# Operand sums of the seven-product gate in the feed-forward stage: traced between gate and up of the first tile pair, from high plus low parts

## The chip, the cores and the metric

The kernel runs on one core of one Trainium2 chip. The metric is the device time of one execution, in microseconds (us). The core has a matrix engine (PE, with its weight loads as PEld), a vector engine (DVE), an activation engine (ACT), a general engine (POOL) and a queue that issues transfers (SP). Matmuls write PSUM banks; everything else lives in SBUF.

## The reference, cut to what matters

Two layers; each has a mixer (three kinds of attention), then the feed-forward stage, then a small embedding stage. Sequence 512, model width 1024, feed-forward width 2816. The change lies in the feed-forward stage:

```python
hn = rms_norm(h, norm_ffn[i])
h = h + (jax.nn.silu(hn @ w_ffn_gate[i]) * (hn @ w_ffn_up[i])) @ w_ffn_down[i]
```

## The kernel before

**Number format.** Every f32 operand of a matmul is split into a high part (a copy to f32r, by ACT) and a low part (whole minus high, by DVE or POOL), and every product is three matmuls (`mm3`): high x high (L223), high x low (L224), low x high (L225).

**Norm.** `norm_T` takes four token tiles of 128 rows (tt 0 to 3), each in two halves of the width (kh 0 and 1). Row statistics run on ACT (squares, L313) and POOL (L322, L335, L336), DVE scales (L369, tile `xn`), PE transposes into a PSUM bank (L382, `xnT`; two such banks), ACT writes the high part (L387) and DVE the low part (L390) of `xT`. In the feed-forward stage ACT also copies the whole from the same bank into f32 tiles `xF` (L393, 8 copies a layer).

**Pairs.** `feed_forward` walks eleven pairs of 128 feed-forward columns (`fp`). Pair 0 computes gate and up directly: 96 matmuls of 256 columns each, first for tokens 0 to 255, then for 256 to 511. From pair 1 on the gate comes from `seven`: seven products of quadrants in place of eight (order 1, 7, 5, 2, 6, 4, 3; 12 matmuls each, 84 in all, tile `st`). Products 1, 2 and 4 read `xT` itself. Products 7, 5, 6 and 3 read sums of the four quadrants of the normed input, quadrant (t, kh) being token half t and width half kh:

X7 = (0,0) - (1,0), X5 = (1,0) + (1,1), X6 = X5 - (0,0), X3 = (0,1) - X6.

`operand_sums` makes them once a layer, each as a whole (DVE, L409, tile `Xw`), a high part (ACT, L411) and a low part (DVE, L412).

**Weights.** Weights land in `wraw` (four buffers). For the direct pairs each is split by `halves` into `whl` (five buffers): high by ACT (L199), low by POOL or DVE in turn (L202). In `seven` the right-hand sides are split at L445 (ACT) and L446 (POOL for products 1, 2, 3, DVE for the others), after differences on DVE (L431, tile `T`). After up, DVE multiplies gate and up (L1246), ACT and POOL split the result (L1247, L1248, tile `hid`).

**Order.** The order on each engine is fixed before the run. Among the instructions whose inputs and buffers are ready in the framework's modelled time, an engine takes the one traced earliest; `prio(n)` moves one n places forward. So later steps run early where an engine would be idle, and what is traced earlier goes first where two are ready. Tiles of `utile` share 15 buffers. In the run itself every engine keeps its order and waits.

Of the kernel before, what the change touches and what calls it, by code (L numbers as in the profile page):

```python
# [10 lines left out]
F32 = mybir.dt.float32  # L11
# [3 lines left out]
AF = mybir.ActivationFunctionType  # L15
ALU = mybir.AluOpType
# [3 lines left out]
P = 128  # L20
S = 512
# [21 lines left out]
def hybrid_trunk_kernel(  # L43
# [12 lines left out]
    te, ve, se, ge = nc.tensor, nc.vector, nc.scalar, nc.gpsimd  # L56
# [5 lines left out]
    def f(ap):  # L62
        return ap.bitcast(F32)
# [8 lines left out]
    def bank(tag, shape=(P, 512), dt=F32, name=None):  # L72
        bufs = {"d": 2, "s": 3, "t": 2, "o": 1}[tag]
        return ps.tile(list(shape), dt, name=name or f"ps_{tag}", tag=tag, bufs=bufs)

    def utile(shape, dt=F32R, name="u"):

        return upool.tile(list(shape), dt, name=name, tag="u", bufs=15)
# [12 lines left out]
    def etile(name="e"):  # L91
        return upool.tile([P, 512], F32, name=name, tag="e", bufs=4)
# [4 lines left out]
    def ptile(name="p"):  # L97
        return upool.tile([P, 512], F32, name=name, tag="p", bufs=6)
# [6 lines left out]


    OFE, OFN, OFP = 100, 50, 200
    KEEP = 150

    def weave(*streams):  # L110

# [8 lines left out]
    def run(*gens):  # L120
        for g in gens:
            for _ in g:
                pass
# [5 lines left out]
    @contextlib.contextmanager  # L129
    def prio(off):  # L130

        c = tc.cur_priority
        tc.cur_priority = c - off
        yield
        tc.cur_priority += off
# [86 lines left out]
    def mm3(acc, lh, ll, rh, rl, start, stop):  # L222
        i = te.matmul(acc, lhsT=lh, rhs=rh, start=start, stop=False, skip_group_check=True)  # L223
        te.matmul(acc, lhsT=lh, rhs=rl, start=False, stop=False, skip_group_check=True)  # L224
        te.matmul(acc, lhsT=ll, rhs=rh, start=False, stop=stop, skip_group_check=True)  # L225
        return i
# [112 lines left out]
    def load_gain(gain):  # L339

        next_gain.append(utile([P, D], F32, name="gx"))
        nc.sync.dma_start(next_gain[0], bc(gain, D))
# [27 lines left out]
                yield tt, kh, xn  # L370
        done.clear()

    def norm_T(keep=None):


        g = next_gain.pop()
        xT = [[utile([P, 4, S], name=f"xT{i}{j}") for j in range(2)] for i in range(2)]
        with prio(OFN if last_act[0] else 5000):
            for tt, kh, xn in normed(g):
                pt = bank("t", (P, 4, P), name="xnT")  # L380
                for j in range(4):
                    te.transpose(pt[:, j, :], xn[:, j * P:(j + 1) * P], ident)  # L382
                hi, lo = (xT[kh][j][:, :, tt * P:(tt + 1) * P] for j in range(2))
                if kh == 0 and "first tile" not in latest:
                    ve.tensor_copy(hi, pt)
                else:
                    last_act[0] = se.activation(hi, pt, AF.Copy)  # L387
                if tt == 0 and kh == 1:
                    latest["first tile"] = last_act[0]
                latest["xT"] = ve.tensor_tensor(lo, pt, f(hi), op=ALU.subtract)  # L390
                if keep:
                    with prio(-KEEP):
                        se.activation(keep[kh][:, :, tt * P:(tt + 1) * P], pt, AF.Copy)  # L393

        def act(k, half, tt=None):
            t = xT[k // 4][half][:, k % 4, :]
            return t if tt is None else t[:, tt * P:(tt + 1) * P]
        return act

    def operand_sums(xact, F):  # L400


        a = [[F[kh][:, :, t * 256:(t + 1) * 256] for kh in range(2)] for t in range(2)]
        X = {}
        for n, (x, y, op) in ((7, (a[0][0], a[1][0], ALU.subtract)), (5, (a[1][0], a[1][1], ALU.add)),
                              (6, (5, a[0][0], ALU.subtract)), (3, (a[0][1], 6, ALU.subtract))):
            whole = utile([P, 4, 256], F32, name="Xw")
            F[n] = whole
            ve.tensor_tensor(whole, *(F[z] if isinstance(z, int) else z for z in (x, y)), op=op)  # L409
            X[n] = t = utile([P, 2, 4, 256], name=f"X{n}")  # L410
            se.activation(t[:, 0], whole, AF.Copy)  # L411
            ve.tensor_tensor(t[:, 1], whole, f(t[:, 0]), op=ALU.subtract)  # L412

        def left(n, half, k):
            if n in X:
                return X[n][:, half, k]
            t, kh = {1: (0, 0), 2: (0, 1), 4: (1, 1)}[n]
            return xact(4 * kh + k, half)[:, t * 256:(t + 1) * 256]
        return left
# [115 lines left out]
    def mixer(i):  # L535
# [316 lines left out]
        def softmaxes(items):  # L852
# [8 lines left out]
            def scores(it):  # L861
# [8 lines left out]
                mx, sm, rc = (small.tile([P, 4], F32, name=x)[:, :k] for x in ("mx", "sm", "rc"))  # L870
                ve.tensor_reduce(mx, sv, axis=AX.X, op=ALU.max, negate=True)  # L871
                it["e"] = e = ptile("p")
# [123 lines left out]
        def cmp_maps(g, pc):  # L996
# [18 lines left out]
            mx = small.tile([P, 16], F32, name="cmx", bufs=2)  # L1015
            ve.tensor_reduce(mx, e3, axis=AX.X, op=ALU.max)
            ve.tensor_tensor(e3, e3, mx[:, :, None].to_broadcast([P, 16, 32]), op=ALU.subtract)
            se.activation(e, e, AF.Exp)
            ve.tensor_tensor(e4, e4, bmask[:, :, None].to_broadcast([P, NT, 4, 32]), op=ALU.mult)
            sm = small.tile([P, 16], F32, name="csm", bufs=2)  # L1020
            ve.tensor_reduce(sm, e3, axis=AX.X, op=ALU.add)
            ve.tensor_scalar(sm, sm, TINY, None, op0=ALU.max)
# [175 lines left out]

    def feed_forward(i, add_h, between):
        lo_turn[0] = 2  # L1200
        F = dict(enumerate(utile([P, 4, S], F32, name=f"xF{j}") for j in range(2)))
        xact = norm_T(F)
        hidden, left = {}, None

        def hact(k, half, tt):
            return hidden[k // 2][:, half, k % 2, tt * P:(tt + 1) * P]

        def units(fp):
            hidden[fp] = hid = utile([P, 2, 2, S], name="hid")
            gate = {}  # L1210

            def gate_done(j, t):
                gate[j] = t
                se.activation(t, t, AF.Silu)

            def part(w, a2, ks, cols):
                for k, (hi, lo) in ks:
                    for j in range(2):
                        cs = slice(j * P, (j + 1) * P)
                        m = mm3(a2[j][:, cols], hi[:, cs], lo[:, cs], xact(k, 0)[:, cols], xact(k, 1)[:, cols],  # L1220
                                k == 0 and cols.start == 0, k == KD - 1)
                        if k == 0 and cols.start == 0:
                            first.append(m.ins)

            for wi, w in enumerate((w_ffn_gate[i], w_ffn_up[i])):
                if left and wi == 0:
                    seven(left, w, fp * 256, "ddss", gate_done)
                    continue
                accs = [bank(t, name=f"gu{wi}{j}") for j, t in enumerate(("dd", "ss" if fp == 0 else "to")[wi])]
                ws = enumerate(weights(w, allk, fp * 256, 256, 2))  # L1230
                first = []
                if fp == 0:

                    ws = list(ws)
                    part(w, accs, ws, slice(0, 256))
                    with tc.issue_after(first[1]):
                        part(w, accs, ws, slice(256, 512))
                else:
                    part(w, accs, ws, slice(0, 512))
                if wi == 0:  # L1240
                    for j in range(2):
                        gate[j] = sg = etile("sg")
                        se.activation(sg, accs[j], AF.Silu)
            for j in range(2):
                sg = gate[j]
                ve.tensor_tensor(sg, sg, accs[j], op=ALU.mult)  # L1246
                se.activation(hid[:, 0, j, :], sg, AF.Copy)  # L1247
                ge.tensor_tensor(hid[:, 1, j, :], sg, f(hid[:, 0, j, :]), op=ALU.subtract)  # L1248


        parts = range(0, 6), range(6, NF // 2)
        for fps in parts:
            for fp in fps:
                units(fp)
                if fp == 0:
                    left = operand_sums(xact, F)
            end = fps is parts[-1]
            kts = list(range(2 * fps[0], 2 * fps[-1] + 2))
            for c, tags in ((0, "ddss"), (512, "stto")):
                if end:  # L1260
                    if c:
                        between()
                    else:
                        load_gain(norm_ple[i])
                run(project(hact, w_ffn_down[i], kts, c, 512, add_h(c, end), tags=tags,
                            tail=4 if end and c else 2))
# [167 lines left out]
```

## Time and profile before

| | |
|---|---|
| median of 3 runs | 1566.41 us (1566.28 to 1570.38) |
| the profiled execution | 1570.22 us, its span 1568.4 us |
| busy PE, DVE, ACT, POOL | 96%, 61%, 51%, 39% of the span |
| granted PE clock, mean | 0.99 of full speed |
| feed-forward stage of layer 1, first pair | from about 356 us |
| feed-forward stage of layer 2, first pair | from about 1129 us |

Times in the rows are from the start of the span. A matmul's busy time overlaps that of its neighbours, since they are pipelined: the pace is the distance of two starts, and a bracket at the end of a line gives the idle time before it and what ended that.

### The profile page before, as it was taken

To read this page: it belongs to the slowest core of one execution; us is meant where nothing else is said; L and a number is where in the kernel's file an instruction comes from. 1 tells how busy PE (TensorE), PEld (TensorE's weight loads), DVE (VectorE), ACT (ScalarE), POOL (GpSimd) and SP (SyncE) were. 2 spreads that over 40 slices of the span, in tenths; PEclk is the share of its full clock that TensorE was granted. 3 is DMA by queue.
4 is the path that set the end of the run, shared out by engine and by line. 5 is a ranking of instruction groups with operands and counts; after the bars stand their busy time and mean duration, and the time that the engine had idled before them with its cause. 6 is when DMAs were issued, how large, how long until landed. Compare 5 with 4: busy or idle time off the path is not lost.

```text
span 1568.4 us, 25192 instructions
## 1 busy us (share of the span) xinstructions
PE 1499.3 (96%) x9346; PEld 1307.9 (83%) x9346; DVE 953.5 (61%) x1840; ACT 800.1 (51%) x1705; POOL 613.7 (39%) x656
## 2 busy tenths in 40 slices
PE   6999999998999999999999999999889999999998
PEld 5898887877898888988988888778789888998888
DVE  6777869766763246534386878797666623654253
ACT  5476666655443234433355767586554432444343
POOL 3323455553344234432233235465434432444323
PEclk9999999999999999999999999999999999999999
DMA  5421321121333323342224131212223333334321
GB/s 174 124 73 42 82 68 34 48 94 58 104 95 99 99 85 108 108 134 68 81 69 123 55 80 44 81 28 64 71 81 95 94 121 95 94 95 132 111 68 54
DMA packets 114458, 134.70 MB, mean 86 GB/s; under 512 B 6864, under 2 KB 91936, under 8 KB 114336
## 3 DMA queue, kind: packets, MB, share of 16 engines
q1 hardware_dynamic: 114336, 133.10, 27.9%
q8 instruction: 74, 1.21, 0.3%
q14 instruction: 48, 0.39, 0.1%
HBM read 122.59 MB, written 2.10 MB: 80 GB/s over the span
## 4 chain that ended last, share of the span: by engine, by line
PE 76%; DVE 13%; ACT 4%; POOL 3%; issue 2%; DMA 1%; POOLq 0%; DVEq 0%; ACTq 0%; SPq 0%
PE acc L223 6%; PE acc L224 6%; PE acc L225 6%; PE gu L225 5%; PE gu L223 5%; PE gu L224 5%; PE st L224 4%; PE st L225 4%; PE st L223 4%; PE accr L223 2%; PE accr L224 2%; PE accr L225 2%; PE sc L866 2%; PE ge L223 2%; PE pTp L887 2%
## 5 line engine op out<-in xcount | busy, mean ns | idle before, releaser
L202 POOL TENSOR_TENSOR whl<-wraw,whl 128x512 fp32r<-128x512 f32 (+2 forms) x208 | 282.4, 1363 | 490.1 <-ACT whl L199 461.2
L199 ACT ACTIVATE whl<-wraw 128x512 fp32r<-128x512 f32 (+2 forms) x336 | 210.1, 631 | 263.6 <-PE acc L225 123.3
L202 DVE TENSOR_TENSOR whl<-wraw,whl 128x512 fp32r<-128x512 f32 x128 | 112.7, 882 | 171.7 <-ACT whl L199 171.3
L224 PE MATMUL gu<-xT,whl 128*128 128x512 f32 (+1 forms) x448 | 161.8, 362 | 0.0
L225 PE MATMUL gu<-xT,whl 128*128 128x512 f32 (+1 forms) x448 | 161.5, 362 | 0.0
L223 PE MATMUL gu<-xT,whl 128*128 128x512 f32 (+1 forms) x448 | 161.1, 361 | 0.0
L446 POOL TENSOR_TENSOR whl<-wraw,whl 128x512 fp32r<-128x512 f32 x60 | 87.1, 1452 | 153.7 <-ACT whl L445 153.6
L223 PE MATMUL acc<-whl,hid 128*128 128x512 f32 x352 | 139.1, 395 | 0.0
L224 PE MATMUL acc<-whl,hid 128*128 128x512 f32 x352 | 139.1, 395 | 0.0
L225 PE MATMUL acc<-whl,hid 128*128 128x512 f32 x352 | 138.8, 394 | 0.0
L446 DVE TENSOR_TENSOR whl<-T,whl 128x512 fp32r<-128x512 f32 x80 | 76.4, 955 | 66.2 <-ACT whl L445 65.6
L879 POOL TENSOR_SCALAR p<-p,rc,gt 128x128 f32<-128x128 f32 (+3 forms) x128 | 79.3, 630 | 71.0 <-DVE rc L877 20.8
L223 PE MATMUL st<-X,whl 128*128 128x256 f32 x320 | 91.5, 286 | 7.9 <-ACT X L411 7.9
L224 PE MATMUL st<-X,whl 128*128 128x256 f32 x320 | 92.1, 288 | 4.3 <-DVE X L412 4.3
L874 ACT ACTIVATE p<-sc,mx 128x128 f32<-128x128 f32 (+3 forms) x160 | 83.9, 535 | 22.7 <-DVE mx L871 20.6
L225 PEld LDWEIGHTS gu<-xT,whl 128*128 128x128 f32 x448 | 84.1, 188 | 13.5
L224 PEld LDWEIGHTS gu<-xT,whl 128*128 128x128 f32 x448 | 84.1, 188 | 13.0
L223 PEld LDWEIGHTS gu<-xT,whl 128*128 128x128 f32 x448 | 84.0, 188 | 12.9
L225 PE MATMUL st<-X,whl 128*128 128x256 f32 x320 | 91.4, 285 | 0.0
L445 ACT ACTIVATE whl<-T 128x512 fp32r<-128x512 f32 x80 | 50.1, 626 | 70.5 <-PE gu L225 57.4
L893 DVE TENSOR_TENSOR pT<-pTp,pT 128x512 fp32r<-128x512 f32 (+2 forms) x120 | 70.5, 596 | 19.5 <-ACT pT L892 18.5
L892 ACT ACTIVATE pT<-pTp 128x512 fp32r<-128x512 f32 (+2 forms) x120 | 62.1, 528 | 38.0 <-PE pTp L887 36.7
(334 smaller groups left out, 4499.4 us busy)
## 6 DMA issues: line engine op xcount, KB each, us to landing
wraw<-in_w_ffn_gate_dram SPq DMA_DIRECT2D x44, 512.0 KB, 3.6
wraw<-in_w_ffn_up_dram SPq DMA_DIRECT2D x44, 512.0 KB, 3.7
wraw<-in_w_ffn_down_dram SPq DMA_DIRECT2D x44, 512.0 KB, 3.8
wraw<-in_w_in_dram SPq DMA_DIRECT2D x36, 512.0 KB, 3.6
wraw<-in_w_out_dram SPq DMA_DIRECT2D x16, 512.0 KB, 3.8
wraw<-in_w_ple_gate_dram SPq DMA_DIRECT2D x16, 512.0 KB, 3.5
sw<-nq SPq DMA_DIRECT2D x32, 128.0 KB, 2.3
wraw<-in_w_in_dram SPq DMA_DIRECT2D x8, 280.0 KB, 2.9
```

What stands on the lines that cost most here:

```text
L199: se.activation(whl[:, 0], raw[:, lo:lo + n], AF.Copy)
L202: eng.tensor_tensor(whl[:, 1], raw[:, lo:lo + n], f(whl[:, 0]), op=ALU.subtract)
L223: i = te.matmul(acc, lhsT=lh, rhs=rh, start=start, stop=False, skip_group_check=True)
L224: te.matmul(acc, lhsT=lh, rhs=rl, start=False, stop=False, skip_group_check=True)
L225: te.matmul(acc, lhsT=ll, rhs=rh, start=False, stop=stop, skip_group_check=True)
L445: se.activation(whl[:, 0], src, AF.Copy)
L446: (ge if n in (1, 2, 3) else ve).tensor_tensor(whl[:, 1], src, f(whl[:, 0]), op=ALU.subtract)
L866: te.matmul(s[:, c:c + w], lhsT=lhsT, rhs=rhs, start=(j == 0), stop=False, skip_group_check=True)
L874: se.activation(e[:, u * n:(u + 1) * n], s[:, u * n:(u + 1) * n], AF.Exp, bias=mx[:, u:u + 1], accum_out=sm[:, u:u + 1])
L879: ge.tensor_scalar(e[:, u * n:(u + 1) * n], e[:, u * n:(u + 1) * n], rc[:, u:u + 1], gates[u] if gates else 1.0, op0=ALU.mult, op1=ALU.mult)
L892: se.activation(hi, src, AF.Copy)
L893: ve.tensor_tensor(lo, src, f(hi), op=ALU.subtract)
```

## The change

The eight copies `xF` at the norm are gone. `operand_sums` is traced right after the first pair's gate (behind its Silu, ahead of its up), where it stood after the whole first pair. It first rebuilds the whole quadrants as high plus low: per width half one instruction on POOL (tokens 0 to 255) and one on DVE (tokens 256 to 511), 128x1024 each. Then come the same four sums with the same splits. The wholes are put in two buffers instead of four.

```diff
@@ -105,7 +105,6 @@
 
 
     OFE, OFN, OFP = 100, 50, 200
-    KEEP = 150
 
     def weave(*streams):
 
@@ -370,8 +369,7 @@
                 yield tt, kh, xn
         done.clear()
 
-    def norm_T(keep=None):
-
+    def norm_T():
 
         g = next_gain.pop()
         xT = [[utile([P, 4, S], name=f"xT{i}{j}") for j in range(2)] for i in range(2)]
@@ -388,28 +386,33 @@
                 if tt == 0 and kh == 1:
                     latest["first tile"] = last_act[0]
                 latest["xT"] = ve.tensor_tensor(lo, pt, f(hi), op=ALU.subtract)
-                if keep:
-                    with prio(-KEEP):
-                        se.activation(keep[kh][:, :, tt * P:(tt + 1) * P], pt, AF.Copy)
 
         def act(k, half, tt=None):
             t = xT[k // 4][half][:, k % 4, :]
             return t if tt is None else t[:, tt * P:(tt + 1) * P]
+        act.tiles = xT
         return act
 
-    def operand_sums(xact, F):
-
-
-        a = [[F[kh][:, :, t * 256:(t + 1) * 256] for kh in range(2)] for t in range(2)]
-        X = {}
-        for n, (x, y, op) in ((7, (a[0][0], a[1][0], ALU.subtract)), (5, (a[1][0], a[1][1], ALU.add)),
-                              (6, (5, a[0][0], ALU.subtract)), (3, (a[0][1], 6, ALU.subtract))):
-            whole = utile([P, 4, 256], F32, name="Xw")
-            F[n] = whole
-            ve.tensor_tensor(whole, *(F[z] if isinstance(z, int) else z for z in (x, y)), op=op)
-            X[n] = t = utile([P, 2, 4, 256], name=f"X{n}")
-            se.activation(t[:, 0], whole, AF.Copy)
-            ve.tensor_tensor(t[:, 1], whole, f(t[:, 0]), op=ALU.subtract)
+    def operand_sums(xact):
+
+
+        X, whole = {}, {}
+
+        for kh in range(2):
+            F = utile([P, 2, 4, 256], F32, name="xF")
+            for t in range(2):
+                hi, lo = (xact.tiles[kh][j][:, :, t * 256:(t + 1) * 256] for j in range(2))
+                whole[t, kh] = F[:, t]
+                (ve if t else ge).tensor_tensor(F[:, t], f(hi), f(lo), op=ALU.add)
+        for pair in (((7, (0, 0), (1, 0), ALU.subtract), (5, (1, 0), (1, 1), ALU.add)),
+                     ((6, 5, (0, 0), ALU.subtract), (3, (0, 1), 6, ALU.subtract))):
+            W = utile([P, 2, 4, 256], F32, name="Xw")
+            for j, (n, x, y, op) in enumerate(pair):
+                whole[n] = W[:, j]
+                ve.tensor_tensor(W[:, j], whole[x], whole[y], op=op)
+                X[n] = t = utile([P, 2, 4, 256], name=f"X{n}")
+                se.activation(t[:, 0], W[:, j], AF.Copy)
+                ve.tensor_tensor(t[:, 1], W[:, j], f(t[:, 0]), op=ALU.subtract)
 
         def left(n, half, k):
             if n in X:
@@ -1198,9 +1201,8 @@
 
     def feed_forward(i, add_h, between):
         lo_turn[0] = 2
-        F = dict(enumerate(utile([P, 4, S], F32, name=f"xF{j}") for j in range(2)))
-        xact = norm_T(F)
-        hidden, left = {}, None
+        xact = norm_T()
+        hidden, left = {}, []
 
         def hact(k, half, tt):
             return hidden[k // 2][:, half, k % 2, tt * P:(tt + 1) * P]
@@ -1223,8 +1225,8 @@
                             first.append(m.ins)
 
             for wi, w in enumerate((w_ffn_gate[i], w_ffn_up[i])):
-                if left and wi == 0:
-                    seven(left, w, fp * 256, "ddss", gate_done)
+                if fp and wi == 0:
+                    seven(left[0], w, fp * 256, "ddss", gate_done)
                     continue
                 accs = [bank(t, name=f"gu{wi}{j}") for j, t in enumerate(("dd", "ss" if fp == 0 else "to")[wi])]
                 ws = enumerate(weights(w, allk, fp * 256, 256, 2))
@@ -1241,6 +1243,8 @@
                     for j in range(2):
                         gate[j] = sg = etile("sg")
                         se.activation(sg, accs[j], AF.Silu)
+                if fp == 0 and wi == 0:
+                    left.append(operand_sums(xact))
             for j in range(2):
                 sg = gate[j]
                 ve.tensor_tensor(sg, sg, accs[j], op=ALU.mult)
@@ -1252,8 +1256,6 @@
         for fps in parts:
             for fp in fps:
                 units(fp)
-                if fp == 0:
-                    left = operand_sums(xact, F)
             end = fps is parts[-1]
             kts = list(range(2 * fps[0], 2 * fps[-1] + 2))
             for c, tags in ((0, "ddss"), (512, "stto")):
```

## Rows read from the trace of the kernel before

**Rows 1.** Page, part 1: busy time, share of the span, instructions.

```profile
PE 1499.3 (96%) x9346; PEld 1307.9 (83%) x9346; DVE 953.5 (61%) x1840; ACT 800.1 (51%) x1705; POOL 613.7 (39%) x656
```

**Rows 2.** Timeline of PE, first `seven` of layer 1: start, duration, what, [idle before].

```profile
386.68 0.39 PE L223 MATMUL st<-X,whl 128*128 128x256 f32 x1 [0.73 <-ACT X L411]
390.27 0.58 PE L223 MATMUL st<-X,whl 128*128 128x256 f32 x1 [3.21 <-ACT X L411]
391.40 0.58 PE L224 MATMUL st<-X,whl 128*128 128x256 f32 x1 [0.55 <-DVE X L412]
...
400.20 0.39 PE L224 MATMUL st<-X,whl 128*128 128x256 f32 x1 [1.51 <-DVE X L412]
```

**Rows 3.** Windows, `st` on PE alone: length, busy (count), clock, DMA share, GB/s.

```profile
382.96:403.48 20.52, 13.29 (x84) 0.83 0.20 61
1155.75:1175.66 19.91, 12.49 (x84) 0.91 0.21 61
413.14:423.04 9.90, 9.89 (x84) 1.00 0.24 73
```

**Rows 4.** Windows: length, then busy (count) of PE, PEld, DVE, ACT, POOL, clock.

```profile
371.77:382.96 11.19, 11.19 (x97) 11.19 (x96) 1.54 (x3) 4.20 (x7) 2.61 (x3) 1.00 0.47 147
...
386.80:391.40 4.60, 0.85 (x2) 0.35 (x2) 4.60 (x5) 1.41 (x2) 3.46 (x2) 0.74 0.23 64
391.40:395.80 4.40, 4.40 (x20) 4.40 (x21) 2.82 (x3) 1.65 (x3) 0.00 (x0) 0.50 0.37 117
```

**Rows 5.** Timeline of DVE, layer 1, from the last norm step on.

```profile
367.16 0.69 DVE L390 TENSOR_TENSOR xT<-xnT,xT 128x512 fp32r<-128x512 f32 x1 [0.55 <-ACT xT L387]
369.84 0.69 DVE L202 TENSOR_TENSOR whl<-wraw,whl 128x512 fp32r<-128x512 f32 x1 [1.98 <-ACT whl L199]
379.58 0.69 DVE L446 TENSOR_TENSOR whl<-T,whl 128x512 fp32r<-128x512 f32 x1 [9.05 <-ACT whl L445]
...
384.01 1.22 DVE L409 TENSOR_TENSOR Xw<-xF 128x1024 f32<-128x1024 f32 x1
...
386.85 2.28 DVE L409 TENSOR_TENSOR Xw<-xF,xF 128x1024 f32<-128x1024 f32 x1
```

**Rows 6.** Timeline of POOL, layer 1: splits.

```profile
371.25 1.31 POOL L202 TENSOR_TENSOR whl<-wraw,whl 128x512 fp32r<-128x512 f32 x1 [1.51 <-ACT whl L199]
...
384.45 3.60 POOL L1248 TENSOR_TENSOR hid<-sg,hid 128x512 fp32r<-128x512 f32 x2 [0.69 <-ACT hid L1247]
388.01 2.25 POOL L446 TENSOR_TENSOR whl<-wraw,whl 128x512 fp32r<-128x512 f32 x1
```

**Rows 7.** Lines of tile `we`, other stage: 128x1024 alone, ns min/median/max.

```profile
L202 DVE TENSOR_TENSOR we<-wraw,we x2: 1224/1225/1226, 673.1 to 1445.2; 128x1024 fp32r<-128x1024 f32 x2
L202 POOL TENSOR_TENSOR we<-wraw,we x2: 2398/2401/2404, 679.4 to 1451.3; 128x1024 fp32r<-128x1024 f32 x2
```

**Rows 8.** Lines L411 and L393: ns min/median/max of one, first and last start.

```profile
L411 ACT ACTIVATE X<-Xw x8: 1038/1046/1057, 385.6 to 1170.6; 128x1024 fp32r<-128x1024 f32 x8
L393 ACT ACTIVATE xF<-xnT x16: 579/594/602, 352.2 to 1141.1; 128x512 f32<-128x512 f32 x16
```

**Rows 9.** PE around a late low half (its split is DVE's line).

```profile
398.29 0.40 PE L224 MATMUL gu<-xT,whl 128*128 128x512 f32 x1
400.07 0.68 DVE L202 TENSOR_TENSOR whl<-wraw,whl 128x512 fp32r<-128x512 f32 x1
401.72 0.62 PE L225 MATMUL gu<-xT,whl 128*128 128x512 f32 x2
```

**Rows 10.** Norm of layer 1: ACT copy and square, waits of PE's transposes.

```profile
356.70 0.59 ACT L393 ACTIVATE xF<-xnT 128x512 f32<-128x512 f32 x1
357.18 0.63 ACT L313 ACTIVATE junk<-h 128x512 bf16<-128x512 f32 x1
359.81 0.63 PE L382 MATMUL xnT<-ident,xn 128*128 128x128 f32 x4 [0.81 <-DVE xn L369]
364.02 0.63 PE L382 MATMUL xnT<-ident,xn 128*128 128x128 f32 x4 [0.90 <-DVE xn L369]
```

## The prediction

> **What bounds the kernel now.** I read the page's busy times first: PE is busy for 96% of the span [rows 1], so a gain can only come from places where PE waits or runs slowly, and work taken from the other engines counts for nothing in itself. Next I read the waits of PE by tile. The tile `st` of the seven products stands out, and the timeline of PE shows where: in the first `seven` of a layer PE stops three times for the high parts of the operand sums (L411) and for their low parts (L412), the longest time for 3.21 us, and a fourth time for 1.51 us [rows 2]. The reader should see that products 1 and 2, which read `xT`, have run by then, and that the stops are at the first matmuls that read `X`.
>
> What the stops cost is read by setting windows side by side. The 84 matmuls of a later `seven` take 9.90 us; the first of layer 1 takes 20.52 us and the first of layer 2 19.91 us [rows 3]. Six matmuls of up (512 columns, so twice the 9.90 / 84 = 0.118 us of one of 256) lie within each of the two, 1.4 us. So the sums cost 20.52 - 9.90 - 1.4 = 9.2 us in layer 1 and 8.6 us in layer 2, 17.8 us together, 1.1% of the time. Not all of it is waiting: behind the long stop the granted clock is 0.50, that is 1.2 instead of 2.4 GHz, and 20 matmuls take 4.40 us [rows 4], against 20 x 0.118 = 2.4 us at full clock. So 2.0 us of the 9.2 are a slow clock that followed a stop.
>
> Why are the sums late? They are traced behind the whole first pair, and DVE starts them only at 384 [rows 5], when up is done. Right before, during up, DVE is busy for 1.54 us of 11.19, ACT for 4.20, POOL for 2.61 [rows 4], and DVE stands idle for 9.05 us in one piece [rows 5]. Their inputs are complete from 367.85 on, when the last low part of `xT` ends [rows 5].
>
> **The change part by part.** *Copies removed.* Sixteen ACT instructions of 594 ns are gone [rows 8], 9.5 us of ACT, off PE's path. One reaches it: a copy at 356.70 runs ahead of the square at 357.18, on which the next tile's statistics wait [rows 10]. Without it that tile's chain is up to 0.48 us earlier.
>
> *Wholes rebuilt.* A layer gets two 128x1024 sums on POOL, 2.40 us each, and two on DVE, 1.22 us each [rows 7]. The POOL ones need only token tiles 0 and 1, so they can start in the middle of the norm, when POOL still has the statistics of tiles 2 and 3 to do. A whole that has started holds them. Bounds per layer: 0.5 us of gain (the copy gone, POOL's sums in gaps) to 2.4 us of loss (one whole straight ahead of a statistic that PE waits for). PE waits 0.81 us at tile 2 and 0.90 us at tile 3 [rows 10]; what tile 2 loses, the wait of tile 3 takes up, so I take 0.3 us of loss. That POOL does half of this is a choice on which the Trainium skill has a rule: GPSIMD Engine Reference, section Engine selection, gives elementwise sums of a tile to VectorE because POOL takes about twice as long for two inputs. The trace agrees on the ratio, 2401 to 1224 ns [rows 7]. By that rule both POOL sums would go to DVE, which would lengthen the DVE queue costed next by 2.4 us; by the rows that queue is the one that is short of time, so here I hold the rule to be the worse choice.
>
> *The sums moved.* The queue that matters is DVE: two wholes, four sums, four low parts, ten instructions of 1.22 us, 12.2 us. The first fits in front of the last low part of `xT`, from about 366.6 (0.55 us of idle before 367.16, [rows 5]); with that part's 0.69 the ten end near 379.5. ACT has four copies of 1.05 us [rows 8] and room for them [rows 4]. Product 7 is due at about 384.4 (12 x 0.118 behind the start of `seven` at 382.96), so X7 and X5, first in the queue, are early, and X6 and X3 are ready long before products 6 and 3. The stops of [rows 2] go, and with them the slow clock: 9.2 and 8.6 us.
>
> *What is queued behind them.* The sums are now traced ahead of up's weight splits. Three of up's four splits fall into this time: two on POOL (1.31 us, [rows 6]), one, for the third quarter of the weights, on DVE at 369.84 [rows 5]. That one will stand behind the sums and end not at 370.5 but near 379.5 + 0.7 = 380.2. Moreover DVE and POOL slow each other: a sum that takes 1.22 us alone takes 2.28 us while POOL works [rows 5, 6], and a POOL split 2.25 instead of 1.31 [rows 6]. Three POOL splits (two of up, one of product 1) lie beside the sums, 3 x 1.06 = 3.2 us, so the DVE split ends nearer to 383.4.
>
> PE needs that low half for 8 of up's 96 matmuls only. The trace shows that PE's order goes round such a gap: at 398.29 it runs the high-half matmuls of up, and their two L225 come at 401.72, behind the late split on DVE at 400.07 [rows 9]. So the cost has two ends per layer: nothing, if the 8 matmuls stand last (up ends at 382.96 anyhow), or, if the order was fixed for 380.2 and the split comes at 383.4, a wait of 3.2 us and 2.0 us of slow clock behind it, as in [rows 4], 5.2 us. [Rows 9] lie nearer to the low end, but nothing shows DVE so full at this place; I take the middle, 2.6 us.
>
> *The rest* costs nothing that I can find. The `seven` splits at L446 on DVE come behind the queue, but product 1 is split by POOL and product 7 has until 384.4; the cover is those first 12 matmuls, 1.4 us, and a later end would show as a wait of the same length at product 7. SP issues the same loads. The 15 shared buffers carry 4 (`xT`) + 2 + 2 + 4 (`X`) + 1 (`hid`) = 13 at most where it was 15.
>
> *Sum.* 17.8 - 2 x (2.6 + 0.3) = 12.0 us gained. The profiled execution took 1570.2 us, so it would take 1558.2; the median lies 3.8 us below that execution, so 1554.4 is the forecast in terms of the median.
>
> **The rivals.** *Everything gained.* The splits find their gaps or PE goes round them: 17.8 - 0.6 = 17.2 us, 1549. For it: [rows 9] and 11 us of nearly idle engines; against it: ten DVE instructions fill that time to the last us.
>
> *Gain eaten, no change.* If PE keeps the order of the weights, it reaches the third quarter after 24 matmuls, at 371.77 + 2.8 = 374.6. A split that ends at 381.2 then costs 6.6 us of waiting, 2.0 of clock and 0.3 in the norm, as much as the 8.9 gained: 1566. The case that the sums don't move, since a buffer or an input holds them, gives the same time; the count of buffers and the 367.85 above speak against it.
>
> *Slower.* The same mechanism in its place, up's third quarter behind the sums on DVE with PE waiting in order of the weights, decides for slower by more than 0.3% (about 4.7 us, what a measurement of this kernel can tell from no change) once the split ends after 383.5. It gets there if POOL's wholes run late, beside DVE's sums: two of 2.40 us are 3.7 splits' worth, 3.7 x 1.06 = 3.9 us more, an end at 387.3, a wait of 12.7 us, 14.7 with the clock: 2 x (14.7 + 0.3 - 8.9) = 12 us lost, 1578. Against it: [rows 9], and that POOL has idle time before 367.
>
> **How the numbers follow.** Forecast (1550 to 1562) 0.56; everything gained 0.20; no change 0.16; slower 0.08. So faster by over 0.3% 0.76, within 0.3% 0.16, slower 0.08. The bounds of the unknown terms give 17.8 + 1.0 = 18.8 us gained at best, 1547.6, and 17.8 - 2 x (5.2 + 2.4) = 2.6 us at worst, 1563.8: the range is 1547 to 1564. It leaves out the slower case and part of no change.
>
> **What would show it.** In the profile after: no wait of `st` on L411 or L412, the first `seven` of each layer in about 10 us (plus what up fills in), a clock of 1.00 there; the sums on DVE between 366 and 384; the third-quarter split on DVE past 378, and a wait of up's L225 for it if that term is real. The norm's two waits at the transposes show POOL's share. The prediction is wrong if up waits more than 6 us in a layer, if the clock falls in up, or if time is lost in stages that the change doesn't touch, through another order of the work behind it.

## The result and the profile after

Over six runs each, the kernel before took 1570.31 us (1566.28 to 1573.08) and the changed one 1558.53 us (1555.70 to 1560.10): a ratio of 0.9926, with a 95% interval of 0.9906 to 0.9946. That is 11.8 us less, where 12.0 us less was forecast. The forecast in absolute terms, 1554.4, stood on the first three runs of before, whose median was 3.9 us lower than that of all six.

First the busy times, as in [rows 1]:

```profile
PE 1499.2 (96%) x9346; PEld 1309.6 (84%) x9346; DVE 954.3 (61%) x1844; ACT 792.3 (51%) x1689; POOL 624.7 (40%) x660
```

PE does the same 9346 matmuls in the same busy time. ACT is 7.8 us lighter, since its 16 copies are gone, and POOL 11 us heavier. Nothing in these sums tells of the gain.

The windows of the first `seven` of each layer, `st` on PE alone, as in [rows 3] (length, busy and count, clock, DMA share, GB/s), show where it is:

```profile
385.91:396.10 10.19, 10.18 (x84) 1.00 0.14 35
1154.32:1164.40 10.08, 10.08 (x84) 1.00 0.14 34
```

The 84 matmuls now run without a stop at full clock, in 10.2 and 10.1 us, where it was 20.52 and 19.91. The four stops of [rows 2] are gone. But `seven` starts 29.57 us after the first matmul of gate in layer 1 (356.34 to 385.91) and 29.72 us in layer 2 (1124.60 to 1154.32), where it was 26.72 and 26.68 in the kernel before: some 2.9 and 3.0 us are given back ahead of it. The place is the norm, and the timeline of PE (layer 1, then layer 2) shows it, beside [rows 10]:

```profile
363.09 0.63 PE L380 MATMUL xnT<-ident,xn 128*128 128x128 f32 x4 [3.24 <-DVE xn L368]
...
1131.37 0.63 PE L380 MATMUL xnT<-ident,xn 128*128 128x128 f32 x4 [3.31 <-DVE xn L368]
```

PE waits once for 3.2 us at the third token tile, where it waited 0.81 and 0.90 at the third and the fourth. DVE waits in turn for POOL. POOL's timeline of layer 1, with the scaling on DVE behind it:

```profile
356.21 2.41 POOL L406 TENSOR_TENSOR xF<-xT,xT 128x1024 f32<-128x1024 f32 x1 [3.33 <-DVE xT L388]
358.70 0.22 POOL L321 TENSOR_SCALAR msr<-ss 128x1 f32<-128x1 f32 x1
359.00 2.36 POOL L406 TENSOR_TENSOR xF<-xT,xT 128x1024 f32<-128x1024 f32 x1
361.32 0.19 POOL L334 TENSOR_TENSOR rsr<-msr,ss 128x1 f32<-128x1 f32 x1
361.59 0.57 POOL L335 TENSOR_TENSOR rsr<-rsr,mhalf 128x1 f32<-128x1 f32 x1
...
362.19 1.41 DVE L368 SCALAR_TENSOR_TENSOR xn<-h,rsr,gx 128x512 f32<-128x512 f32 x2 [3.45 <-POOL rsr L335]
```

The reader should see the order on POOL: the statistic of the third tile (L334, L335) stands behind both rebuilt wholes (L406) and runs at 361.32. In the kernel before it ran at 358.05:

```profile
358.05 0.19 POOL L335 TENSOR_TENSOR rsr<-msr,ss 128x1 f32<-128x1 f32 x1 [1.51 <-ACT junk L313]
```

Behind the wait, the clock is at half its level for some time. The windows have the columns of [rows 4]:

```profile
359.00:364.00 5.00, 1.76 (x16) 1.50 (x15) 1.41 (x2) 0.82 (x3) 4.67 (x6) 1.00 0.00 0
364.30:368.00 3.70, 3.70 (x21) 3.70 (x20) 3.21 (x5) 0.84 (x3) 0.00 (x1) 0.54 0.00 0
```

So a layer loses 3.24 - 1.71 = 1.5 us of waiting and 3.70 x (1 - 0.54) = 1.7 us of slow clock, about what the later start of `seven` shows. The account by the trace: 17.8 us of stalls gone, less 0.3 and 0.2 (windows of 10.19 and 10.08 against 9.90), less 2.85 and 3.04, gives 11.4 us; the medians say 11.8, the two profiled executions (1570.2 and 1560.1) 10.1. The 1.3 us between the account and these two lie outside the two stages: from 815 to 845 us, far from the change, the mean granted clock was 0.83 in the profile after and 0.89 in the one before.

### The profile page after: what moved, and what is told of

Same layout as the page of the kernel before. It is cut to its first block, busy times and chain, and to the rows that moved or that the text cites. A ratio compares the mean times of both kernels' runs of the same rounds, so it can differ in the third digit from the quotient of the medians.

```text
span 1558.4 us, 25196 instructions
## 1 busy us (share of the span) xinstructions
PE 1499.2 (96%) x9346; PEld 1309.6 (84%) x9346; DVE 954.3 (61%) x1844; ACT 792.3 (51%) x1689; POOL 624.7 (40%) x660
## 4 chain that ended last, share of the span: by engine, by line
PE 78%; DVE 11%; POOL 4%; ACT 3%; issue 2%; DMA 0%; POOLq 0%; ACTq 0%; DVEq 0%
PE acc L222 6%; PE acc L223 6%; PE acc L224 6%; PE gu L224 6%; PE gu L223 6%; PE gu L222 6%; PE st L223 4%; PE st L222 4%; PE st L224 4%; PE accr L222 2%; PE sc L869 2%; PE accr L223 2%; PE accr L224 2%; PE ge L222 2%; PE pTp L890 2%
## 5 line engine op out<-in xcount | busy, mean ns | idle before, releaser
L201 DVE TENSOR_TENSOR whl<-wraw,whl 128x512 fp32r<-128x512 f32 x128 | 109.1, 854 | 171.5 <-ACT whl L198 171.2
L224 PEld LDWEIGHTS gu<-xT,whl 128*128 128x128 f32 x448 | 85.2, 190 | 13.7
L223 PEld LDWEIGHTS gu<-xT,whl 128*128 128x128 f32 x448 | 85.1, 190 | 13.2
L222 PEld LDWEIGHTS gu<-xT,whl 128*128 128x128 f32 x448 | 85.1, 191 | 12.9
L222 PE MATMUL st<-X,whl 128*128 128x256 f32 x320 | 89.8, 281 | 0.0
L223 PE MATMUL st<-X,whl 128*128 128x256 f32 x320 | 89.9, 281 | 0.0
L224 PE MATMUL st<-X,whl 128*128 128x256 f32 x320 | 89.7, 280 | 0.0
L224 PEld LDWEIGHTS acc<-whl,hid 128*128 128x128 f32 x352 | 66.4, 189 | 15.4
```

The source lines that it names most:

```text
L201: eng.tensor_tensor(whl[:, 1], raw[:, lo:lo + n], f(whl[:, 0]), op=ALU.subtract)
```

## The experiments

Four questions were open: which half of the change brings the gain, whether POOL's wholes are what holds the norm, why the sums were late in the kernel before, and what up pays when its split on DVE really is late. All nine kernels compute the whole reference. Ratios are against the kernel before, run on the same chip.

**1. The sums moved, the copies kept.** The kernel before, with the call at its new place and nothing else:

```diff
+                if fp == 0 and wi == 0:
+                    left.append(operand_sums(xact, F))
...
-                if fp == 0:
-                    left = operand_sums(xact, F)
```

> The kernel before with one step of the change alone: the sums are traced between gate and up, still from the copies made at the norm, so POOL gets no wholes. Theory (POOL's two wholes hold the row statistics of the norm, 2.85 us a layer, and the move gives all of the gain): the norm is as before, the first seven takes about 10.2 us as after the change, so some 17 us below before, near 1553, 5 us below the changed kernel. Rival (the copies delay the start of the sums, and the rebuilding is what lets them start early): the stops stay in part, 1558 or more.

It took 1554.47 us, 0.9882 [0.9869, 0.9896]. PE at the norm, layer 1, and the first sum on DVE:

```profile
361.17 0.63 PE L382 MATMUL xnT<-ident,xn 128*128 128x128 f32 x4 [0.84 <-DVE xn L369]
365.38 0.63 PE L382 MATMUL xnT<-ident,xn 128*128 128x128 f32 x4 [0.89 <-DVE xn L369]
...
368.03 1.22 DVE L409 TENSOR_TENSOR Xw<-xF 128x1024 f32<-128x1024 f32 x1
```

The norm waits are those of [rows 10], `seven` starts 26.73 us after gate (26.70 in layer 2), as in the kernel before, and its 84 matmuls run through in 9.9 and 9.8 us. The gain, 17 to 18 us, is the whole of the stalls. So the move alone does all the good, and the rebuilding of the wholes costs 4.1 us by the medians, 6.9 by the ratios.

**2. The wholes rebuilt, the sums at their old place.** The changed kernel with the call put back behind the first pair:

```diff
-                if fp == 0 and wi == 0:
-                    left.append(operand_sums(xact))
...
+                if fp == 0:
+                    left.append(operand_sums(xact))
```

> The changed kernel with the call put back behind the first pair: wholes from high plus low, but traced at the old place. Theory: the stops of the first seven come back (17.8 us), and if POOL's wholes still run in the middle of the norm, 5.7 us on top of before: 1570 to 1576. Rival (the rebuilding itself brings the gain, whatever the place): near 1558.

It took 1582.23 us, 1.0068 [1.0055, 1.0081]: slower than the kernel before, and more so than expected, for another reason than expected. POOL, DVE and PE of layer 1:

```profile
383.01 2.39 POOL L406 TENSOR_TENSOR xF<-xT,xT 128x1024 f32<-128x1024 f32 x1
383.30 5.38 DVE L406 TENSOR_TENSOR xF<-xT,xT 128x1024 f32<-128x1024 f32 x2
...
392.03 0.58 PE L222 MATMUL st<-X,whl 128*128 128x256 f32 x1 [6.79 <-ACT X L414]
```

The norm lost nothing here, since the wholes too ran only at 383, although their inputs were there some 16 us earlier, when the last low part of `xT` ended at 366.6. Four more instructions in front of the sums then lengthened the first stop of [rows 2] from 0.73 to 6.79 us. The wholes were a loss at the new place and at the old; and something holds these instructions until 383, which experiments 5 and 7 look for.

**3. POOL's wholes behind the statistics.** In the changed kernel the two wholes wait for the last statistic:

```diff
-                (ve if t else ge).tensor_tensor(F[:, t], f(hi), f(lo), op=ALU.add)
+                with ExitStack() if t else tc.issue_after(latest["pow"].ins):
+                    (ve if t else ge).tensor_tensor(F[:, t], f(hi), f(lo), op=ALU.add)
```

> The changed kernel with POOL's two wholes placed behind the last row statistic of the norm on POOL's queue; nothing else. Theory: PE's wait at the third token tile falls from 3.24 us to about 0.8 and the slow clock behind it goes, 2.85 us a layer: near 1553. Rival (the long wait has another cause, as ACT's order without the copies): the wait stays, 1558. A second rival: the wholes now run beside DVE's sums, each slowing the other, and the time comes back as a wait in up or in the seven: 1558 with the wait in another place.

It took 1562.33 us, 0.9943 [0.9931, 0.9955]: the time did not come back. POOL, DVE and PE:

```profile
363.82 5.10 POOL L407 TENSOR_TENSOR xF<-xT,xT 128x1024 f32<-128x1024 f32 x2
363.88 5.58 DVE L368 SCALAR_TENSOR_TENSOR xn<-h,rsr,gx 128x512 f32<-128x512 f32 x2 [0.38 <-POOL rsr L335]
...
360.32 0.63 PE L380 MATMUL xnT<-ident,xn 128*128 128x128 f32 x4 [0.31 <-DVE xn L368]
366.86 0.63 PE L380 MATMUL xnT<-ident,xn 128*128 128x128 f32 x4 [2.51 <-DVE xn L368]
369.62 1.09 PE L380 MATMUL xnT<-ident,xn 128*128 128x128 f32 x4 [2.01 <-DVE xn L368]
```

At the third tile the theory holds: PE waits 0.31 us. But the wholes now run exactly beside the last scaling on DVE, two instructions that take 1.41 us together in the changed kernel and 5.58 here. PE waits 2.51 and 2.01 us at the fourth tile instead. The queue on POOL was the cause in the changed kernel; out of that queue, the same two wholes are in the way of the scaling that runs beside them.

**4. All wholes on DVE.**

```diff
-                (ve if t else ge).tensor_tensor(F[:, t], f(hi), f(lo), op=ALU.add)
+                ve.tensor_tensor(F[:, t], f(hi), f(lo), op=ALU.add)
```

> The changed kernel with all four wholes on DVE, none on POOL. Theory: the norm's waits go back to those of before, two DVE wholes of 1.22 us fit into DVE's gaps in the norm: near 1553 to 1555. Rival (DVE is the queue that is short, as the prediction argued for POOL): the sums end 2.4 us later and up or product 6 waits: 1558 or more.

It took 1558.83 us, 0.9917 [0.9905, 0.9929], the same as the changed kernel. At the norm PE waits 0.33 and 0.24 us, less than in [rows 10], so without POOL's wholes the missing copies do give 1.1 us a layer. They are spent in up, as PE and POOL show:

```profile
374.97 0.38 PE L224 MATMUL gu<-xT,whl 128*128 128x256 f32 x1 [2.65 <-POOL whl L201]
...
368.59 8.05 POOL L201 TENSOR_TENSOR whl<-wraw,whl 128x512 fp32r<-128x512 f32 x2 [5.50 <-ACT whl L198]
```

Two splits that take 1.31 us each alone [rows 6] take 8.05 us together beside an uninterrupted DVE, and up waits for them.

**5. Rank alone.** The kernel before, its sums at the old place but 400 places ahead in order:

```diff
-                    left = operand_sums(xact, F)
+                    with prio(400):
+                        left = operand_sums(xact, F)
```

> The kernel before, its sums traced at the old place but given the precedence of instructions 400 places earlier, so that they rank ahead of up's splits. Theory (the sums were late because of their rank): they start near 369 in layer 1 and the stops go, near 1553. Rival (they were late because their tiles are handed out in order of tracing, behind the tile of the first pair's result, which is first written at 383.8): they still start at 384 and the time is that of before, 1570.

It took 1568.58 us, 0.9979 [0.9966, 0.9992]. DVE of layer 1:

```profile
379.48 0.69 DVE L446 TENSOR_TENSOR whl<-T,whl 128x512 fp32r<-128x512 f32 x1 [9.04 <-ACT whl L445]
...
383.91 1.22 DVE L409 TENSOR_TENSOR Xw<-xF 128x1024 f32<-128x1024 f32 x1
```

The idle piece of 9 us is still there and the first sum still starts at 383.9. The sums came in another order among themselves, which may be the little that was gained. So their place in the order of tracing was not what kept them: with a rank 400 places ahead, on an idle engine, with their inputs there, they did not start.

**6. Up's splits behind the sums.** The changed kernel, with up's splits issued after the last low part of the sums, to have the wait that the prediction feared:

```diff
+                    with tc.issue_after(latest["sums"].ins) if wi else ExitStack():
+                        ws = list(ws)
```

> The changed kernel with up's two DVE splits of the first pair placed behind the last of the sums on DVE, to measure the term that the prediction set at 2.6 us a layer between 0 and 5.2. If PE goes round the late low halves: no wait in up, within 1 us of the changed kernel, 1558. If PE waits for them: up to 5 us a layer, 1563 to 1568.

It took 1585.39 us, 1.0095 [1.0081, 1.0109], 13 us a layer more than the changed kernel and far more than was expected. DVE and PE:

```profile
386.44 1.29 DVE L201 TENSOR_TENSOR whl<-wraw,whl 128x512 fp32r<-128x512 f32 x2
...
379.48 0.58 PE L222 MATMUL st<-xT,whl 128*128 128x256 f32 x1 [4.57 <-ACT whl L448]
385.83 0.58 PE L222 MATMUL st<-X,whl 128*128 128x256 f32 x1 [1.94 <-ACT whl L448]
387.18 0.79 PE L224 MATMUL gu<-xT,whl 128*128 128x256 f32 x2 [0.55 <-DVE whl L201]
```

PE does go round the gap, and even takes products of `seven` first; but there is not enough other work, and it waits 4.57, 1.13, 1.94 and 0.55 us, with a granted clock of 0.50 from 379.5 to 388. What the edit held in the run is both of up's splits on DVE, the first quarter's and the third's (x2 at 386.44; POOL's two still ran at 371.06 and 375.64). So twice as many products were held as the prediction had feared, and the run bounds the price from above.

**7. The buffer of `hid` written early.** The kernel before, with one column of the first pair's `hid` set to zero when the pair begins (it is overwritten later):

```diff
             hidden[fp] = hid = utile([P, 2, 2, S], name="hid")
+            if fp == 0:
+                ge.memset(f(hid[:, 0, 0, 0:1]), 0.0)
```

> The kernel before with one instruction more per layer: POOL writes one column of the first pair's result tile (hid) at the start of that pair, so that this tile is taken early; the sums stay at the old place and rank. Theory (the sums were late only because the tiles of the shared buffers are handed out in order of tracing, and hid, traced ahead of them, was first written at 383.8): the sums start near 368 in layer 1, behind up's splits where both are ready, the stops go and nothing is added at the norm: 1553 to 1555, as the run with the move alone. Rival (the place in the trace matters for another reason): they start at 384 and the time is 1570.

It took 1550.09 us, 0.9867 [0.9854, 0.9880], the lowest median here, clear of the changed kernel. POOL, DVE and PE, layer 1:

```profile
352.65 0.10 POOL L1211 MEMSET hid<- 128x1 f32 x1
...
366.62 1.23 DVE L409 TENSOR_TENSOR Xw<-xF 128x1024 f32<-128x1024 f32 x1
370.68 0.68 DVE L202 TENSOR_TENSOR whl<-wraw,whl 128x512 fp32r<-128x512 f32 x1
...
359.75 0.63 PE L382 MATMUL xnT<-ident,xn 128*128 128x128 f32 x4 [0.83 <-DVE xn L369]
363.96 0.63 PE L382 MATMUL xnT<-ident,xn 128*128 128x128 f32 x4 [0.90 <-DVE xn L369]
```

An instruction of 0.10 us lets the sums start at 366.62 instead of 384.01, at their old place in the trace and at their old rank. That shows what held them: `hid`, whose first write is traced ahead of the sums and ran only behind up. The reading that fits experiments 1, 2, 5 and 7 is that tiles of `utile` get their 15 buffers in the order in which their first writes are traced, so that the sums' tiles had to wait for that of `hid`. In the changed kernel the sums are traced ahead of that write, which has the same effect. The saving is 21 us; 17.8 are the stalls. The rest goes with the clock far from the change (825 to 850 us: 1.00 in this profile, 0.86 in the kernel before), and its interval overlaps that of experiment 1. Run by run the two are alike at the same mean granted clock: at 0.990 experiment 1 took 1554.3 and 1554.6 us and experiment 7 1554.1, at 0.994 they took 1549.4 and 1550.7. So experiment 7 is not shown to be the faster of the two.

**8. POOL and DVE exchanged.** The changed kernel, tokens 0 to 255 on DVE and 256 to 511 on POOL:

```diff
-                (ve if t else ge).tensor_tensor(F[:, t], f(hi), f(lo), op=ALU.add)
+                (ge if t else ve).tensor_tensor(F[:, t], f(hi), f(lo), op=ALU.add)
```

> The changed kernel with the token halves of the wholes swapped: DVE makes those of tokens 0 to 255, which are ready in the middle of the norm, POOL those of 256 to 511, which are ready only when the norm is done. If POOL's wholes cost time because they come ahead of the row statistics: PE's wait of 3.3 us at the third tile falls below 1 us, 2.85 us a layer or more come back; POOL then has 2 x 2.4 us ahead of up's splits, which may give 1 to 2 us of that back: 1551 to 1556. If the sharing of SBUF between POOL and DVE costs more than the order: POOL's splits end late and up waits 2.5 us or more a layer, 1558 or more.

It took 1568.63 us, 0.9981 [0.9971, 0.9991]. POOL, DVE and PE:

```profile
366.93 5.21 POOL L406 TENSOR_TENSOR xF<-xT,xT 128x1024 f32<-128x1024 f32 x2 [3.26 <-DVE xT L388]
380.49 0.68 DVE L201 TENSOR_TENSOR whl<-wraw,whl 128x512 fp32r<-128x512 f32 x1
...
374.43 0.39 PE L224 MATMUL gu<-xT,whl 128*128 128x256 f32 x1 [1.53 <-POOL whl L201]
381.22 0.80 PE L224 MATMUL gu<-xT,whl 128*128 128x256 f32 x2 [4.87 <-DVE whl L201]
```

The norm is free (0.32 and 0.24 us), but the wholes now push up's splits: the one on DVE runs at 380.49, the time that the prediction had named for the changed kernel, and PE waits 4.87 us for it, in both layers. This is the prediction's second rival, seen on the chip: it had a split that ends at 381.2 cost 6.6 us of waiting and 8.9 us a layer in all. Here the split ends at 381.17, PE waits 1.53 + 4.87 = 6.40 us in up, and `seven` starts 34.75 us after gate, 8.0 later than in the kernel before.

**9. Early buffer, old place, wholes on DVE.** Experiments 2, 4 and 7 together:

```diff
-                (ve if t else ge).tensor_tensor(F[:, t], f(hi), f(lo), op=ALU.add)
+                ve.tensor_tensor(F[:, t], f(hi), f(lo), op=ALU.add)
...
+            if fp == 0:
+                ge.memset(f(hid[:, 0, 0, 0:1]), 0.0)
...
-                if fp == 0 and wi == 0:
-                    left.append(operand_sums(xact))
...
+                if fp == 0:
+                    left.append(operand_sums(xact))
```

> Wholes from high plus low, all four on DVE, no copies at the norm, the sums traced behind the first pair as before, and the result tile of the first pair taken early by a one-column write. Up's splits now rank ahead of the sums. If the run with all wholes on DVE lost 2.65 us a layer only because its sums ranked ahead of up's splits: no wait in up, the short norm waits of that run (0.6 us instead of 1.7), near 1551. If it lost them because DVE's steady two-input work slows POOL's splits whatever the rank: the wait in up stays, 1556 to 1559.

It took 1561.36 us, 0.9933 [0.9919, 0.9947]. POOL, DVE and PE:

```profile
369.15 6.31 POOL L201 TENSOR_TENSOR whl<-wraw,whl 128x512 fp32r<-128x512 f32 x1 [5.50 <-ACT whl L198]
...
369.62 1.22 DVE L412 TENSOR_TENSOR Xw<-xF 128x1024 f32<-128x1024 f32 x1
371.35 1.22 DVE L412 TENSOR_TENSOR Xw<-xF 128x1024 f32<-128x1024 f32 x1
...
375.52 0.38 PE L224 MATMUL gu<-xT,whl 128*128 128x256 f32 x1 [2.63 <-POOL whl L201]
```

The splits of up now rank ahead of the sums, and PE waits 2.63 us all the same: what makes the POOL split late is not the order but the company. One split takes 6.31 us, while the three 128x1024 instructions of DVE that start and end beside it keep their 1.22.

## Why the prediction was right, and where its terms were wrong

Of the 12.0 us that were forecast 11.8 were measured, and the first step held. Two of the later terms were wrong, in opposite directions, and cancelled: they stood at 2 x (2.6 + 0.3) = 5.8 us, and 2.85 + 3.04 = 5.9 were lost, all of it where the smaller term had been. That the sum came out so close is luck.

**What bounds the kernel: right.** The 17.8 us of stops and slow clock read from [rows 2 to 4] are what experiment 1 gains (17.3 us by its medians), and the changed kernel shows the two windows of 10 us that the prediction asked for.

**Why the sums were late: half right.** The prediction put it to their place in the trace alone. Experiment 5 shows that rank did not help, experiment 7 that the buffer of `hid` did. Counting 15 buffers of 15 was the right look at the wrong moment: the question was not how many tiles live at once, but who is served first. For the time of the changed kernel the two explanations give the same; for the engineer they don't, since experiment 7 has the gain without any rebuilding.

**Copies removed: right in sign, too small.** Taken as up to 0.48 us. Where POOL's wholes are out of the way (experiments 4, 8 and 9) PE waits some 0.57 us at the norm in place of the 1.71 of [rows 10], 1.1 us a layer less. In the changed kernel none of it is seen.

**Wholes rebuilt: mis-sized, and outside its bound.** Taken as 0.3 us a layer with an end at 2.4; it was 2.9 and 3.0. The mechanism was named, a whole straight ahead of a statistic that PE waits for. The step that failed is "what tile 2 loses, the wait of tile 3 takes up": both wholes ran ahead of the third tile's statistic, so that PE lost more than the two waits together had been, and the prediction counted no slow clock there, though it had read one behind a wait of the same length, 3.21 us, in [rows 4]. By the waits and the clock the loss is 1.5 + 1.7 us.

**Up's split on DVE: the term was 0, not 2.6.** The timeline of DVE in the changed kernel, with the copy on ACT whose lateness made the gap:

```profile
369.75 2.35 DVE L406 TENSOR_TENSOR xF<-xT,xT 128x1024 f32<-128x1024 f32 x2
372.02 3.48 DVE L412 TENSOR_TENSOR Xw<-xF 128x1024 f32<-128x1024 f32 x2
375.42 0.68 DVE L201 TENSOR_TENSOR whl<-wraw,whl 128x512 fp32r<-128x512 f32 x1
376.02 1.21 DVE L415 TENSOR_TENSOR X<-Xw,X 128x1024 fp32r<-128x1024 f32 x1
...
374.40 1.06 ACT L414 ACTIVATE X<-Xw 128x1024 fp32r<-128x1024 f32 x1 [1.63 <-DVE Xw L412]
```

The split did not stand behind all ten instructions, as the prediction had it (end at 380.2 to 383.4), but behind four (two wholes and two sums), and ran at 375.42, ahead of X7's low part, whose high part ACT began only at 374.40. The order leaves a gap where a low part waits for its high part, and the split was ready. PE did not wait in up at all. The reasons given for a small price were not the ones that held: experiment 8 has the split at 380.49, and up alone pays some 9 us a layer there (8.0 net of the 1.1 gained at the norm), 6.40 of them in waiting and most of the rest in a clock of 0.50 from 381.2 to 386.0, more than the 5.2 of the upper bound; and in experiment 6, with two splits held back, PE goes round the gap only in part and pays 13 us a layer. [Rows 9] showed two matmuls waiting in a stage with much other work; that didn't carry over to eight here.

**The rivals.** *Everything gained* is what the move alone does, 17.2 forecast and 17.3 measured in experiment 1; the rebuilding kept the change from it. *No change* had its mechanism right and its price nearly (8.9 us a layer forecast, 8.0 in experiment 8), and *slower* its mechanism, in experiment 6; the changed kernel never got there. The rule of engine choice that the prediction weighed came out even: with all wholes on DVE, as the Trainium skill has it (GPSIMD Engine Reference, Engine selection), the time is 1558.83, with half of them on POOL 1558.53. I had held it the worse choice; the runs don't bear that out, and they don't bear the rule out either. Each way pays at another place.

**Left open.** Why the granted clock differs from run to run in stretches far from the change; the medians of experiments 1 and 7 differ with it.

## What to carry to other kernels

When work stands late on an idle engine, ask first what it waits for besides its inputs: here it was, by the reading that fits experiments 1, 2, 5 and 7, a buffer that was promised to a tile not yet written, and an early write of one column was worth more than the whole rearrangement. When work is put into idle time, list what each of its engines still owes in that stretch, and price a wait on PE with the slow clock behind it: here 3.2 us of waiting cost about 5. Two parts of one change are best costed and run apart: one of these brought 17 us, the other took 4 to 7 back.

## What the runs showed of the hardware

**POOL and DVE slow each other unevenly.** With two inputs in SBUF on both sides, a POOL split of 128x512 took 1.31 us alone, 1.90 and 2.36 beside the sums of the changed kernel, and up to 6.31 beside an unbroken row of DVE sums (experiment 9), while those sums kept 1.22 us (in the changed kernel the two sums beside the split of 1.90 took 3.48 together). In experiment 3 it was DVE that paid: two scalings took 5.58 us in place of 1.41, beside POOL instructions of 2.55 each (2.36 to 2.41 in the changed kernel). The timeline of POOL in the changed kernel:

```profile
371.38 1.90 POOL L201 TENSOR_TENSOR whl<-wraw,whl 128x512 fp32r<-128x512 f32 x1 [7.08 <-ACT whl L198]
376.06 2.36 POOL L201 TENSOR_TENSOR whl<-wraw,whl 128x512 fp32r<-128x512 f32 x1 [2.77 <-ACT whl L198]
```

The Trainium skill (GPSIMD Engine Reference, Specifications) says that POOL shares its SBUF interfaces with VectorE and that they contend when DVE's instruction has two SBUF inputs. The runs agree and add the size, up to a factor of 4 to 5, and that either side can be the one that pays.

**A wait of 3.2 us was followed by half the clock for longer than it had lasted.** Behind the 3.24 us in which PE waited at the norm, the granted clock was 0.54 for the next 3.70 us (1.2 GHz for most of it); [rows 4] have 0.50 for 4.40 us behind 3.21. A wait of 3.2 us thus cost about 5. Shorter waits went either way: behind the 2.63 us of experiment 9 (layer 1) it was 0.56 for 3.50 us, behind the 2.65 us of experiment 4 (layer 1) it stayed at 1.00 for 3.60 us.
